# Strassen for the queries and keys of all pairs ahead of attention, with casts on GpSimd, biased exponentials in the recurrence and stored token sums for the gates

## The chip, the cores and the metric

The kernel runs on one core of a Trainium2 chip. The metric is the device time of one execution in microseconds, lower is better. The kernel before was timed in three runs, with a median of 1444.59 us (1444.48 to 1446.14).

## What is computed

The reference is one layer of a hybrid encoder on x of 1024 tokens by 1024 features, in float32. Cut to what matters:

```python
q_a, k_a, v_a, f_a, q_b, f_b, i_b, g_b, gate_a, gate_b = split(x @ w_in)
# 8 heads of 64: forgetting attention
F = cumsum(log_sigmoid(f_a + b_f), over tokens)
p = softmax(where(causal, q_a @ k_a.T / sqrt(64) + F[t] - F[s], -inf))
y_a = p @ v_a
# 4 heads of 128 x 128: gated linear recurrence, in chunks of 64 tokens
f = lb + (1 - lb) * sigmoid(f_b); k = 1 - f; b = cumsum(log f) in the chunk
S_new = exp(b_last) * S + (k * exp(b_last - b)).T @ i_b
o_b = (silu(q_b) * exp(b)) @ S + within_chunk(silu(q_b), k, b) @ i_b
y_b = rms_norm(o_b) * norm_g * sigmoid(g_b)
merged = sigmoid(gate_a) * (y_a @ w_pa) + sigmoid(gate_b) * (y_b @ w_pb)
x = layer_norm(ALPHA * x + merged @ w_o)
u, g = split(x @ w_ff_in)                    # 2 x 2816 hidden features
x = layer_norm(ALPHA * x + (silu(g) * u) @ w_ff_out)
```

## The kernel before

Every matmul operand is split into a high and a low fp32r half, and a product takes three matmuls (`mm3`: high by high, high by low, low by high). The high half is a cast on ScalarE, the low half a subtraction on VectorE (`split`). The v projection, the q and k of the first pair of heads, most of the gates and both FFN products use one level of Strassen: seven products of half size in place of eight, with sums of weights and of tokens before them and sums of results after them.

The program is not issued in the order of the code. Every call goes into `Plan`, which knows a cost for each instruction and what depends on what. `schedule` lists the calls on each engine by due times that `latest` works out backwards, `improve` repeats the two `ROUNDS` times and keeps the best, and `issue` emits a fixed order for each engine. For this reason all instructions of the profile carry one line, L363, and are told apart by the names of their tiles. SyncE issues every DMA, and its queue is such a fixed order too. Matmuls that are needed only later serve as filler: `plan.early` moves their due times, so that they can stand between those of a stage that waits on itself.

The stages, with the names of their tiles:

- The v projection by Strassen (banks `vx`, `vy`), and the forget gates (`forget_gates`, `forget_sums`), which leave the decays, running sums of log f, in DRAM (`nf_d`). The token sums of Strassen (`vops["p5"]`, `"p6"`, `"p7"`, `"p3"`, as high and low halves) are made here from x.
- q and k. `qk_first` makes pair 0 by Strassen, ahead of attention (`qk_s`, `qk_pt`). `qk_project` makes pairs 1 to 3 plainly, one after another, as filler in the attention of the pair before (`qps`, `kps`; weights `wq`, `wk`). `qk_heads` forms from a bank the tiles q2, k2 and kl of two heads: in q2 one half of the partitions holds the high part of q and the other the low part, k2 holds the high part of k twice, kl its low part.
- Attention, pair by pair. Per head, a row of decays is loaded into two quarters of `box1` (row r plain, row r+1 with the causal mask added by VectorE); two heads alternate. Scores (`s`), a softmax in 8 blocks of queries (`p`, with the sum in `soft`; GpSimd scales by the reciprocal), transposes (`pt`) and the weighted sum (`pv`). The plainly made gate columns (`gps`, `ge`) are filler here too.
- The recurrence of 4 heads (`bps` projections, `lp`, `up`, `op`, `ot`, `kdt`), `hgrn`. The forget factor `hbf` is made by a VectorE tensor_scalar, and the decayed keys `kd` from a difference with the block's total `tot` and four exponentials of 128x512.
- The gates by Strassen (`GatePair`, banks `gs`, operands `gs1` to `gs4`, weights `Tgp`). Their token sums are formed anew from x (`xg_r`) by `sums4`.
- The branch projections (`pps`), the output projection (`o`), layer norm, FFN in (`fa` to `fd`) and FFN out (`p`).

Of the kernel before, what the change touches and what calls it, by code (L numbers as in the profile page):

```python
# [34 lines left out]
ROUNDS = 20  # L35
MARGIN = 1.06
SLACK = 400.0
SWITCH = 300.0
ALPHA = 2.0 ** 0.25
# [16 lines left out]

class Plan:
# [4 lines left out]
    OWN = {"PE": 0.0, "ACT": 0.0, "DVE": 127.0, "POOL": 60.0, "SP": 2500.0}  # L62
    SETS = {AF.Exp: 0, AF.Ln: 0, AF.Sigmoid: 1, AF.Silu: 2}

    def __init__(self, tc):
        self.tc = tc
        self.calls, self.tiles, self.log, self.first = [], {}, {}, {}
        self.queues, self.rank = {}, []
        self.early = 0
        self.loose = set()  # L70

# [22 lines left out]
    def add(self, q, method, args, kw):  # L94
# [7 lines left out]
        if method == "copy_predicated":  # L102
            ins.append(outs[0])
        n = len(self.calls)
        self.rank.append(n - self.early)
        pred = set()
# [21 lines left out]
        both = sum(str(v.space).endswith("SB") and v.free_size() > 128 for v in ins) > 1  # L128
        self.calls.append((q, method, args, kw, pred, names, fresh, self.cost(q.name, method, outs, ins, kw), both))

    def cost(self, eng, method, outs, ins, kw):
# [27 lines left out]
        if eng == "POOL":  # L159
            if method == "tensor_tensor" and kw.get("op") == ALU.pow:  # L160
# [9 lines left out]
    def schedule(self, slack, wait):  # L170
# [13 lines left out]
        dma_free = 0.0  # L184
        fifo, slots = {}, {}
# [15 lines left out]
        while done < len(calls):  # L201
            best = None
            for q, av in avail.items():
                for i in av:
# [16 lines left out]
                    if not ok:  # L221
                        continue
                    if q == "ACT":
# [14 lines left out]
            if q == "SP":  # L238
                start = max(t + 100, dma_free)
                dma_free = start + d  # L240
                free[q] = t + 60
                fin = dma_free
            else:
# [6 lines left out]
                fin = t + d  # L250
                free[q] = fin
# [35 lines left out]
    def lag(self, i, u, slack):  # L287
        q, uq = self.calls[i][0].name, self.calls[u][0].name
        lat = self.OWN[q] if uq == q else self.LAT[q]
# [4 lines left out]
    def latest(self, slack):  # L294
# [7 lines left out]
        for old, i in self.after:  # L302
            for m in by.get(old, ()):
                users[m].append((i, self.LAT[calls[m][0].name] + 60))
# [29 lines left out]
    def improve(self, slack, wait):  # L334
# [4 lines left out]
        for _ in range(ROUNDS):  # L339
            last, self.rank = self.turn, self.latest(slack)  # L340
# [26 lines left out]
def trunk(ctx: ExitStack, tc, a: dict, out: bass.AP):  # L367
# [30 lines left out]
    def small(shape, name, bufs=4):  # L398
        return plan.tile(cst, shape, F32, "c_" + name, name, bufs)
# [67 lines left out]

    def operand1(tag, name):
# [3 lines left out]
    def operand4(tags, name):  # L472
        ts = [[take(tags[2 * i + j], [2, NB], f"{name}{'hl'[i]}{j}", F32R) for j in range(2)] for i in range(2)]
        return [[ts[i][c // 2][:, c % 2, :] for c in range(4)] for i in range(2)]
# [109 lines left out]
    def forget_gates():  # L584

        LO, NC = 32, KC + 4
        wfx = keep([P, NC, HA], "wfx", F32, "lnst")
# [49 lines left out]
    bf = const("bf", [NT * HA, 1])  # L637
# [29 lines left out]
    causal = const("causal", [P, 2, P], BF16, "mask")  # L667
# [40 lines left out]
    def qk_project(p):  # L708
        tiles = qk_tiles(p)
        for b in range(2):  # L710
            plan.early = AHEAD
            w = weights(a["w_qk"][b, p], [KC, P], f"w{'qk'[b]}{p}", 0)
            plan.early = 0
            for hf in range(2):
                o = bank("g", f"{'qk'[b]}ps{p}_{hf}")
                project(o, w, hf)
                qk_heads(b, hf, o, *tiles)
        return tiles

    def qk_first():  # L720

        g, u = (take("hl", [KC, P], f"w{n}0_r") for n in "qk")
        for b, t in enumerate((g, u)):
            sync.dma_start(t, a["w_qk"][b, 0])
        b11, b12, b21, b22 = g[:, :4], u[:, :4], g[:, 4:], u[:, 4:]
        t2 = take("ph", [4, P], "wqk_t2")
        p1, u2, p5 = (half("ph", f"qk0_{i}") for i in ("p1", "u2", "p5"))
        oa, ob, oc = (bank(t, f"qk0_{t}") for t in ("s", "pt", "s"))
        tiles = qk_tiles(0)

        def mul(p, src, o, first):
            T = [take(f"w{x}0" if p in ("p6", "p2", "p7") else "tt", [4, P], f"Tqk{p}{x}", F32R) for x in "hl"]
            split(*T, src)
            more = {} if first else {"skip_group_check": True}
            for c in range(4):
                mm3(o, T[0][:, c], T[1][:, c], vops[p][0][c], vops[p][1][c], first and c == 0, c == 3, more)
# [4 lines left out]
        split4(A21, a21)  # L741
        mul("p1", b11, oa, True)
        act.copy(p1, oa)
        mul("p2", b21, oa, False)
        dve.tensor_sub(t2, b22, b12)
        qk_heads(0, 0, oa, *tiles)
        mul("p6", t2, ob, True)
        dve.tensor_add(u2, ob, p1)
        mul("p3", b22, oc, False)
        dve.tensor_add(u2, oc, u2)  # L750
        qk_heads(1, 0, u2, *tiles)
# [4 lines left out]
        qk_heads(1, 1, p5, *tiles)  # L756
# [3 lines left out]
        qk_heads(0, 1, p1, *tiles)  # L760
        return tiles

    def attention(p, qk):
        q2, k2, kl = qk
        for i in range(2):
# [5 lines left out]
            for hf in range(2):  # L771
                plain, masked = (nfx[:, b0 + 4 * hf:b0 + 4 * hf + 4].rearrange("p (j c) t -> p j c t", c=2) for b0 in (0, NT))
                dve.tensor_add(masked, plain, causal[:, None].to_broadcast([P, 2, 2, P]))
# [4 lines left out]
            for qb in range(NT):  # L778
                n = (qb + 1) * P
                pt = full("pf", f"p{h}_{qb}") if qb > 3 else half("ph", f"p{h}_{qb}")  # L780
                soft = small([P, 5], "soft")
                mn, sm, rs = soft[:, :3], soft[:, 3:4], soft[:, 4:]
# [24 lines left out]
                dve.reciprocal(rs, sm)  # L807
                pool.tensor_scalar(pt[:, :n], pt[:, :n], rs, 1.0, op0=ALU.mult, op1=ALU.mult)
                pr.append(pt)
                if qb % 4 < 3:  # L810
# [26 lines left out]
    ng = const("ng", [P, 1])  # L837
    lbl = const("lbl", [P, HB])
    lbt = keep([P, 4, HB], "lbt")
# [915 lines left out]
```

## Time and profile before

| | |
|---|---|
| Median of 3 runs | 1444.59 us (1444.48 to 1446.14) |
| Span of the profiled execution, first to last instruction | 1441.5 us |
| Granted TensorE clock | 0.998 |
| TensorE matmul, busy | 1430.0 us (99%) |
| VectorE | 1112.8 us (77%) |
| ScalarE | 668.6 us (46%) |
| GpSimd | 87.2 us (6%) |
| DMA, mean over the span | 126 GB/s, 181.30 MB |

The profiled execution is one run of the program; the span leaves out what lies before its first and after its last instruction, and the median of the runs stands 3.1 us above it. A row of instructions reads: line, engine, operation, output tile <- input tiles, shapes, count | busy us in all, mean ns of one | idle time of the engine just before them, and what ended it. The engines are PE (TensorE matmul), PEld (its weight loads), DVE (VectorE), ACT (ScalarE), POOL (GpSimd) and SP (SyncE, which issues DMAs). Buffer numbers are left out of the names, so a row collects all tiles of a kind.

### The profile page before, as it was taken

What the parts mean: (1) busy time and instruction counts of PE and PEld (TensorE: products, weight loads), DVE (VectorE), ACT (ScalarE), POOL (GpSimd) and SP (SyncE); (2) the same over time, 40 slices, a digit from 0 to 9 for tenths busy, and PEclk for the clock granted to TensorE, in tenths of its full rate; (3) what the DMA queues carried; (4) which work ended last, traced back from release to release, by engine and by line L of the source; (5) the groups of instructions that cost most, each with busy time, mean ns of one, the idle gap of its engine ahead of it and who ended that gap; (6) DMA issues with size and microseconds to landing.
All of it is one profiled execution on the core that took longest, in us unless ns stands there. A gap on an engine that the chain in (4) does not pass through costs nothing.

```text
span 1441.5 us, 18901 instructions
## 1 busy us (share of the span) xinstructions
PE 1430.0 (99%) x6782; PEld 1188.2 (82%) x6782; DVE 1112.8 (77%) x1952; ACT 668.6 (46%) x1167; POOL 87.2 (6%) x100
## 2 busy tenths in 40 slices
PE   9999999999999999999999999999999999999997
PEld 7788888888888888788888888888888888888886
DVE  8998778567998999845857997666677776798596
ACT  5547768667767663344511443323333334434330
POOL 0002213120100110000000000000000000000011
PEclk9999999999999999999999999999999999999999
DMA  7022212211111455858500233233333326977632
GB/s 270 32 89 67 95 60 74 63 60 51 38 59 46 153 170 164 255 181 290 176 0 2 102 95 124 96 110 110 110 110 110 97 92 201 346 276 235 209 129 85
DMA packets 74029, 181.30 MB, mean 126 GB/s; under 512 B 8384, under 2 KB 9792, under 8 KB 73936
## 3 DMA queue, kind: packets, MB, share of 16 engines
q1 hardware_dynamic: 73936, 180.11, 37.9%
q8 instruction: 53, 0.87, 0.3%
q14 instruction: 40, 0.33, 0.1%
HBM read 139.90 MB, written 40.17 MB: 125 GB/s over the span
## 4 chain that ended last, share of the span: by engine, by line
PE 97%; DVE 2%; DMA 1%; issue 0%; ACT 0%; SPq 0%; DVEq 0%; ACTq 0%
PE p L363 14%; PE fb L363 12%; PE bps L363 9%; PE fc L363 8%; PE fa L363 8%; PE o L363 6%; PE pps L363 6%; PE gs L363 5%; PE vx L363 4%; PE gps L363 3%; PE s L363 2%; PE pv L363 2%; PE qps L363 2%; PE kps L363 2%; PE vy L363 2%; PE pt L363 2%
## 5 line engine op out<-in xcount | busy, mean ns | idle before, releaser
L363 PE MATMUL p<-dp 128*128 128x512 f32 (+1 forms) x957 | 210.1, 382 | 0.0
L363 PEld LDWEIGHTS p<-dp 128*128 128x128 f32 x957 | 175.1, 188 | 34.8
L363 PE MATMUL fc<-xs,Tp 128*128 128x512 f32 x528 | 127.3, 389 | 0.6 <-ACT Tp L363 0.6
L363 PE MATMUL fb<-xs,Tp 128*128 128x512 f32 x528 | 127.2, 389 | 0.0
L363 PEld LDWEIGHTS fc<-xs,Tp 128*128 128x128 f32 x528 | 99.1, 188 | 21.6 <-ACT Tp L363 1.0
L363 PEld LDWEIGHTS fb<-xs,Tp 128*128 128x128 f32 x528 | 99.1, 188 | 20.5
L363 PE MATMUL fa<-x,Tp 128*128 128x512 f32 x480 | 115.6, 389 | 0.0
L363 ACT CAST Tp<-t 128x512 fp32r<-128x512 f32 x88 | 54.2, 619 | 118.8 <-PE fc L363 64.8
L363 DVE TENSOR_TENSOR Tp<-t,Tp 128x512 fp32r<-128x512 f32 x88 | 60.6, 690 | 60.5 <-ACT Tp L363 59.9
L363 PEld LDWEIGHTS fa<-x,Tp 128*128 128x128 f32 x480 | 90.1, 188 | 18.7
L363 PE MATMUL bps<-xh,wb_h 128*128 128x512 f32 x192 | 76.2, 397 | 0.0
L363 PE MATMUL bps<-xl,wb_h 128*128 128x512 f32 x192 | 76.0, 396 | 0.0
L363 PE MATMUL bps<-xh,wb_l 128*128 128x512 f32 x192 | 75.5, 396 | 0.0
L363 POOL TENSOR_TENSOR norm<-norm,mhalf 128x1 f32<-128x1 f32 x16 | 17.2, 1075 | 886.3 <-DVE norm L363 886.3
L363 ACT CAST dp<-dap 128x1024 fp32r<-128x1024 f32 (+1 forms) x42 | 41.0, 979 | 57.8 <-PE p L363 35.7
L363 POOL TENSOR_SCALAR p<-p,soft 128x384 f32<-128x384 f32 (+4 forms) x64 | 51.9, 817 | 261.0 <-DVE soft L363 235.2
L363 DVE TENSOR_TENSOR tl<-pt,th 128x512 fp32r<-128x512 f32 (+1 forms) x96 | 52.2, 554 | 19.7 <-ACT th L363 15.5
L363 ACT CAST th<-pt 128x512 fp32r<-128x512 f32 (+1 forms) x96 | 45.5, 479 | 34.9 <-PE pt L363 30.8
L363 DVE TENSOR_TENSOR dp<-dap,dp 128x1024 fp32r<-128x1024 f32 (+1 forms) x42 | 47.4, 1132 | 15.9 <-ACT dp L363 15.7
L363 PE MATMUL fb<-x,Tp 128*128 128x512 f32 x240 | 57.7, 389 | 0.0
L363 PE MATMUL pt<-ident,p 128*128 128x128 f32 x288 | 53.8, 273 | 0.0
L363 ACT CAST Tp<-wg_r 128x512 fp32r<-128x512 f32 x40 | 24.9, 623 | 62.1 <-PE fb L363 30.2
(565 smaller groups left out, 3476.6 us busy)
## 6 DMA issues: line engine op xcount, KB each, us to landing
dbp<-in_w_fo SPq DMA_DIRECT2D x45, 512.0 KB, 5.3
dap<-a_d SPq DMA_DIRECT2D x35, 512.0 KB, 4.3
wg_r<-in_w_ff SPq DMA_DIRECT2D x22, 512.0 KB, 4.0
wu_r<-in_w_ff SPq DMA_DIRECT2D x22, 512.0 KB, 3.6
a_d<-ar SPq DMA_DIRECT2D x42, 256.0 KB, 2.7
a_d<-as SPq DMA_DIRECT2D x33, 256.0 KB, 3.4
wg_r<-in_w_g SPq DMA_DIRECT2D x16, 512.0 KB, 4.4
sg<-gate_d SPq DMA_DIRECT2D x32, 256.0 KB, 3.4
```

What stands on the lines that cost most here:

```text
L363: getattr(q.engine, method)(*args, **kw)
```

## The change

Six parts:

1. `qk_first` makes q and k of all four pairs by Strassen (`qk_strassen`), in the order 1, 2, 3, 0, ahead of attention. Pair 0 goes to its tiles as before. The results of pairs 1 to 3 go to DRAM (`qk_d`), each 64x512 block written twice, so that a load of 128x512 brings it to both halves of the partitions. `qk_load` reads them a pair ahead: GpSimd makes the high parts by tensor_scalar, VectorE the low parts. `qk_project` is gone.
2. The masked decay row is a load of the causal mask, now 128x1024 float32, and a DMA from GpSimd's queue that adds the decays to it in flight; VectorE's 16 additions are gone.
3. The softmax's reciprocals are taken for three blocks and then one, and the scalings are issued after them. Small constants share one tile (`few`).
4. In the recurrence ScalarE makes `hbf` with scale and bias, and the decayed keys are exponentials with the block's total as bias, 8 of 128x128 per head, without VectorE's difference.
5. The token sums of the v projection are written to DRAM (`sum_d`) and loaded again for the gates, in place of loads of x and `sums4`.
6. The planner has a cost for DMAs of GpSimd's queue, counts 500 ns for an issue on SyncE in place of 60, and runs 24 rounds with a varied slack; the first Silu of the FFN waits for the first token sums there.

The core of the diff:

```diff
-ROUNDS = 20
+ROUNDS = 24
...
-            self.rank = self.latest(slack)
+            self.rank = self.latest(slack if n < 6 else slack * vary.uniform(0, 3))
...
-                free[q] = t + 60
+                free[q] = t + 500
...
+    for n, x in enumerate((xh, xl)):
+        sync.dma_start(sum_d[0, :, n], f(x[0][:, :, hs(1)]))
+    for m, p in enumerate(("p6", "p7", "p3")):
+        for n in range(2):
+            for j in range(2):
+                sync.dma_start(sum_d[m + 1, :, n, 2 * j:2 * j + 2], f(vtiles[...][n][j]))
...
+        def put(b, hf, o):
+            if tiles:
+                return qk_heads(b, hf, o, *tiles())
+            if o is oa:
+                t = half("gt", f"qk{p}_o")
+                act.copy(t, o)
+                o = t
+            for i in range(2):
+                for j in range(2):
+                    sync.dma_start(qk_d[p, b, i, j, :, hs(hf)], o[i * DH:(i + 1) * DH])
...
+    def qk_load(p):
+        q2, k2, kl = qk_tiles(p)
+        for b in range(2):
+            for hf in range(2):
+                for i in range(2):
+                    ot = slice((1 - i) * DH, (2 - i) * DH)
+                    raw = half(f"w{'hl'[i]}0", f"qkr{p}_{b}{hf}{i}")
+                    sync.dma_start(raw, qk_d[p, b, i, :, :, hs(hf)].rearrange("j d t -> (j d) t"))
+                    if b == 0:
+                        pool.tensor_scalar(q2[i][:, hs(hf)], raw, -0.125, None, op0=ALU.mult)
+                        dve.scalar_tensor_tensor(q2[i][ot, hs(hf)], raw[ot], -0.125, f(q2[i])[ot, hs(hf)],
+                                                 op0=ALU.mult, op1=ALU.subtract)
+                    else:
+                        pool.tensor_scalar(k2[i][:, hs(hf)], raw, 1.0, None, op0=ALU.mult)
+                        dve.tensor_sub(kl[i][:, hs(hf)], raw, f(k2[i])[:, hs(hf)])
+        return q2, k2, kl
...
+        for p, w, b in ((1, "hl", 0), (2, "kb", 1), (3, "hl", 0), (0, "kb", 1)):
+            qk_strassen(p, (w, w), (("s", "pt", "s"), ("h", "pv", "h"))[b], None if p else tiles)
...
-            for hf in range(2):
-                plain, masked = (...)
-                dve.tensor_add(masked, plain, causal[:, None].to_broadcast([P, 2, 2, P]))
+            sync.dma_start(box1[:, r + 1, :], a["causal"])
+            pool.dma_start(box1[:, r + 1, :], nf_d[h].partition_broadcast(P), accum_op=ALU.add)
...
-                dve.reciprocal(rs, sm)
-                pool.tensor_scalar(pt[:, :n], pt[:, :n], rs, 1.0, op0=ALU.mult, op1=ALU.mult)
+                if qb % 4 > 1:
+                    lo = 0 if qb % 4 == 2 else 3
+                    dve.reciprocal(sums[:, 4 + lo:5 + qb % 4], sums[:, lo:1 + qb % 4])
+                    for j in range(qb - qb % 4 + lo, qb + 1):
+                        pool.tensor_scalar(pr[j][:, :w], pr[j][:, :w], rs, 1.0, op0=ALU.mult, op1=ALU.mult)
...
-        dve.tensor_scalar(fk, fk, olb[:, h:h + 1], lb[:, h:h + 1], op0=ALU.mult, op1=ALU.add)
+        act.activation(fk, fk, AF.Identity, scale=olb[:, h:h + 1], bias=lb[:, h:h + 1])
...
-            dve.tensor_sub(kd..., bw, tot...)
-            act.activation(qeb[:, odd], kd[:, odd], AF.Exp, scale=-1.0)
-            act.activation(kd[:, even], kd[:, even], AF.Exp, scale=-1.0)
+            for j in range(4):
+                for c, t in enumerate((kd, qeb)):
+                    w = blk(4 * c + j)
+                    act.activation(t[:, w], b[:, w], AF.Exp, bias=tot[:, j, c:c + 1], scale=-1.0)
...
-    gops["p6"] = operand1("m", "gs2")
-    sums4(gops["p6"], q22, q22, q11, True)
+    gops["p6"] = reload(1, "m", "gs2")
```

The planner then places everything anew. Three places show what moved.

TensorE, in attention, at the first transposes of head 1 (`pt1_0_0`). Before, the filler among them is the plain q projection of pair 1 (`qps1_1`):

```order
L363 MATMUL pt1_0_0_301<-ident_162,p1_0_288 128x128
L363 MATMUL pt1_0_0_301<-ident_162,p1_1_291 128x128
L363 MATMUL pt1_0_0_301<-ident_162,p1_2_294 128x128
L363 MATMUL pv0_1_261<-tl0_1_6_282,vhl0_218 128x256
L363 MATMUL pt1_0_0_301<-ident_162,p1_3_297 128x128
L363 MATMUL qps1_1_368<-xh0_66,wq1_h0_363 128x512
L363 MATMUL qps1_1_368<-xl0_68,wq1_h0_363 128x512
L363 MATMUL pv0_1_261<-th0_1_7_284,vhl0_218 128x128
```

After, it is the plain columns of the gates (`gps`), and the first score of head 2, from pair 1's reloaded tiles, comes 13 rows behind the last of the first four transposes:

```order
L381 MATMUL pt1_0_0_373<-ident_162,p1_3_369 128x128
L381 MATMUL pv0_1_332<-tl0_1_6_353,vhl0_287 128x256
L381 MATMUL gps0_1_0_1196<-xl0_68,wg0_1_h0_1192 128x512
L381 MATMUL pv0_1_332<-th0_1_7_355,vhl0_287 128x128
L381 MATMUL gps0_1_0_1196<-xh0_66,wg0_1_l0_1193 128x512
L381 MATMUL pv0_1_332<-tl0_1_7_356,vhl0_287 128x128
L381 MATMUL gps0_1_0_1196<-xh1_67,wg0_1_h1_1194 128x512
```

All q and k matmuls now stand ahead of the first score.

GpSimd, at head 1 of attention (`p1_*` are its softmax blocks). Before, only scalings stand there:

```order
L363 TENSOR_SCALAR p1_1_291<-p1_1_291,soft_292 128x256
L363 TENSOR_SCALAR p1_2_294<-p1_2_294,soft_295 128x384
L363 TENSOR_SCALAR p1_3_297<-p1_3_297,soft_298 128x512
L363 TENSOR_SCALAR p1_4_314<-p1_4_314,soft_315 128x640
L363 TENSOR_SCALAR p1_5_318<-p1_5_318,soft_319 128x768
```

After, casts of pair 1 (`qkr1`) and the accumulating DMA for head 2's masked row (`box1`) stand between them:

```order
L381 TENSOR_SCALAR k2_1_0_431<-qkr1_100_439 128x512
L381 TENSOR_SCALAR q2_1_1_430<-qkr1_001_436 128x512
L381 TENSOR_SCALAR p1_0_360<-p1_0_360,sums_359 128x128
L381 TENSOR_SCALAR p1_1_363<-p1_1_363,sums_359 128x256
L381 TENSOR_SCALAR p1_2_366<-p1_2_366,sums_359 128x384
L381 DMA box1_104<-nf_d_116 128x1024
L381 TENSOR_SCALAR p1_3_369<-p1_3_369,sums_359 128x512
L381 TENSOR_SCALAR k2_1_0_431<-qkr1_110_441 128x512
```

The DMA is issued behind the scaling of block 2 and its softmax sum.

VectorE, at the start of the gates (`Tgp5`, `Tgp6` are low halves of weight sums). Before, sums of tokens (`xg_r`) and low halves of them (`gs`) stand between:

```order
L363 TENSOR_TENSOR Tgp5_4l_1225<-tg1_4_1209,Tgp5_4h_1224 128x512
L363 TENSOR_TENSOR gs1_1223<-xg7_r_1202,gs1_1223 128x512
L363 TENSOR_TENSOR gs2_1228<-xg5_r_1198,gs2_1228 128x512
L363 TENSOR_TENSOR gs2_1228<-xg6_r_1200,gs2_1228 128x512
L363 TENSOR_TENSOR Tgp5_6l_1227<-tg1_6_1219,Tgp5_6h_1226 128x512
L363 TENSOR_TENSOR xg7_r_1202<-xg7_r_1202,xg3_r_1201 128x512
L363 TENSOR_TENSOR gs3l1_1238<-xg2_r_1199,gs3h1_1236 128x512
```

After, only sums and halves of weights, and work for the branch projections (`yr01`) that came forward:

```order
L381 TENSOR_TENSOR Tgp6_4l_1289<-tg2_4_1269,Tgp6_4h_1288 128x512
L381 TENSOR_TENSOR Tgp4_6l_1281<-wg6_r_1252,Tgp4_6h_1280 128x512
L381 TENSOR_TENSOR Tgp5_6l_1286<-tg1_6_1278,Tgp5_6h_1285 128x512
L381 TENSOR_TENSOR Tgp7_4l_1299<-wg5_r_1251,Tgp7_4h_1298 128x512
L381 TENSOR_TENSOR yr01_1395<-yr01_1395,yr11_1396 128x1024
L381 TENSOR_TENSOR Tgp6_6l_1292<-tg2_6_1279,Tgp6_6h_1291 128x512
```

In their place SyncE loads `gs1` to `gs4` from DRAM, each as two transfers of 1 MB (`gs3` as four of 512 KB).

More of the change, by code (lines that the diff above doesn't have):

```diff
@@ L338, in improve @@
         best = self.schedule(slack, wait), self.end, self.times
-        for _ in range(ROUNDS):
-            last, self.rank = self.turn, self.latest(slack)
+        vary = np.random.default_rng(1)
+        for n in range(ROUNDS):
+            last, self.rank = self.turn, self.latest(slack if n < 6 else slack * vary.uniform(0, 3))
             self.turn = self.rank
```

153 lines of the change are left out of this document (87 added, 66 removed).

## The prediction

> **What bounds the kernel now.** I read the page first, then the waits of TensorE, then busy times by stage, then the rows of the instructions that the change touches.
>
> ```profile
> span 1441.5 us, 18901 instructions
> ...
> PE 1430.0 (99%) x6782; PEld 1188.2 (82%) x6782; DVE 1112.8 (77%) x1952; ACT 668.6 (46%) x1167; POOL 87.2 (6%) x100
> ...
> PE 97%; DVE 2%; DMA 1%; issue 0%; ACT 0%; SPq 0%; DVEq 0%; ACTq 0%
> ```
>
> TensorE is busy in 1430.0 of 1441.5 us and carries 97% of the chain that ended last. The waits of TensorE on other engines, over the whole span, are three rows (line waited for; us in total, times, longest):
>
> ```profile
> PE vy L363 <- DVE mhalf L363: 1.2, 1, 1.2
> PE gs L363 <- DVE gu L363: 1.2, 2, 0.8
> PE fc L363 <- ACT Tp L363: 0.6, 1, 0.6
> ```
>
> One is at the start, one in the gates' products, one at the start of the FFN. So the time is the number of matmuls times what one takes, and only two things move it: fewer or more matmuls, and a wait of TensorE that goes or comes. The stages, as busy time of PE, PEld, DVE, ACT, POOL, then granted clock, DMA share, GB/s (5 to 89 us is the v projection, 89 to 112 mostly the q and k of pair 0, 112 to 324 attention, 342 to 542 the recurrence, 542 to 625 the gates):
>
> ```profile
> 5.00:89.00 84.00, 83.88 (x368) 66.14 (x367) 78.48 (x138) 42.66 (x78) 0.00 (x0) 1.00 0.39 134
> 89.00:112.00 23.00, 23.00 (x105) 18.85 (x104) 20.84 (x41) 16.08 (x29) 0.00 (x0) 1.00 0.34 116
> 112.00:324.00 212.00, 211.98 (x1150) 178.35 (x1149) 154.18 (x478) 149.53 (x324) 51.88 (x64) 1.00 0.21 69
> ...
> 342.00:542.00 200.00, 200.00 (x1096) 172.09 (x1095) 181.17 (x291) 138.93 (x261) 16.84 (x14) 1.00 0.28 91
> 542.00:625.00 83.00, 81.83 (x360) 67.19 (x359) 67.92 (x105) 27.23 (x42) 0.00 (x0) 1.00 0.64 192
> ...
> 580.00:600.00 20.00, 19.19 (x85) 15.57 (x84) 16.90 (x25) 5.41 (x8) 0.00 (x0) 1.00 0.97 269
> ```
>
> PE stands still for 0.02 us in 212 us of attention and not at all in 200 us of the recurrence, though VectorE is busy there for 181 of 200 us. VectorE at 91% (23 us of pair 0's Strassen, 20.84 busy) has not cost TensorE anything either. The clock is full everywhere, so no gain can come from it.
>
> **The matmuls that go.** A pair's q and k took 2 x 2 halves x 8 chunks x 3 terms = 96 matmuls of 128x512 in the plain way; by Strassen it is 7 products x 4 chunks x 3 terms = 84. Pair 0 was made so already; for pairs 1 to 3 that is 288 against 252, 36 fewer. What one costs is read from unbroken runs on the chain (start, duration, count):
>
> ```profile
> 103.42 2.72 PE qk_pt L363 x12
> ...
> 211.19 10.88 PE kps L363 x48
> ```
>
> 2.72/12 and 10.88/48 are both 0.2267 us, so a Strassen matmul is as dear as a plain one, and 36 x 0.2267 = **8.16 us** less. No other TensorE work is added: the two copies of the result, the loads and the casts are for other engines. If the old 288 matmuls had covered something that now shows, the cost is a new wait; that is the rest of the sum.
>
> **Ahead of attention.** Three pairs more are made there, 3 x 84 x 0.2267 = 57 us. One pair asks of VectorE 7 low halves, 4 sums of weights and 5 sums of results, 16 instructions at about 0.69 (the kl row below), 11 us beside 19 us of matmuls, which is lighter than what the 89 to 112 row ran without a gap. The order puts matmuls of the next pair into the places where a pair would wait for its own sums. What can be late is the weights: SyncE now issues 8.4 MB of token sums and 6.3 MB of q and k into DRAM here, 14.7 MB. The first row moved 134 GB/s at a share of 0.39, so the full rate is about 134/0.39 = 344 GB/s, and 14.7 MB are 43 us of it, an estimate, in some 100 us that had over 0.6 free. It fits, but weights queued behind these writes may land late: 0 to 2 us. The written data is read much later; its own lateness costs nothing here.
>
> **Attention.** 288 filler matmuls (65.3 us) leave it, and gate matmuls take their place. By the order, TensorE has 159 us of work from the first score to the last weighted sum (212 - 65.3, and 12 us of gate matmuls that moved in). VectorE loses and gains:
>
> ```profile
> L363 DVE TENSOR_TENSOR box<-box,causal 128x512 f32<-128x512 f32 x16 | 10.8, 694 | 0.1
> ...
> L363 DVE RECIPROCAL soft<-soft 128x1 f32<-128x1 f32 x64 | 10.0, 158 | 4.8 <-ACT p L363 4.5
> ...
> L363 DVE SCALAR_TENSOR_TENSOR q<-qps,q 64x512 fp32r<-64x512 f32 x12 | 8.3, 688 | 2.5 <-ACT q L363 2.3
> L363 DVE TENSOR_TENSOR kl<-kps,k 64x512 fp32r<-64x512 f32 x12 | 8.2, 688 | 15.7 <-ACT k L363 15.6
> ...
> L363 DVE TENSOR_TENSOR wk_l<-wk_r,wk_h 128x512 fp32r<-128x512 f32 x6 | 4.7, 778 | 6.7 <-ACT wk_h L363 6.6
> ...
> L363 DVE TENSOR_TENSOR wq_l<-wq_r,wq_h 128x512 fp32r<-128x512 f32 x6 | 4.1, 688 | 0.7 <-ACT wq_h L363 0.6
> ...
> L363 POOL TENSOR_SCALAR p<-p,soft 128x512 f32<-128x512 f32 x8 | 5.9, 733 | 4.8 <-DVE soft L363 3.5 <-PE pt L363 1.0 <-PE s L363 0.3
> ```
>
> Off VectorE go 10.8 (masked rows), 8.3 + 8.2 (halves of q and k), 4.7 + 4.1 (weights' low halves) and 32 x 0.158 = 5.1 (reciprocals, now batched): 41 us. On come 24 low halves at 0.688 = 16.5. So 154.2 - 41 + 16.5 = 130 us in 159, 82% where it was 73%. GpSimd gets 24 casts at 0.733 = 17.6, with 51.9 makes 69 us of 159. Neither is at its end.
>
> But the two engines get in each other's way. In the timeline (start, duration; both inputs of the DVE instructions in SBUF):
>
> ```profile
> 146.01 2.26 POOL L363 TENSOR_SCALAR p<-p,soft 128x896 f32<-128x896 f32 x2 [1.21 <-PE pt L363]
> ...
> 147.59 1.22 DVE L363 TENSOR_TENSOR wk_l<-wk_r,wk_h 128x512 fp32r<-128x512 f32 x1
> ...
> 197.11 1.13 POOL L363 TENSOR_SCALAR p<-p,soft 128x1024 f32<-128x1024 f32 x1 [0.54 <-DVE soft L363]
> 197.46 1.32 DVE L363 TENSOR_TENSOR vhl<-va,vhl 128x512 fp32r<-128x512 f32 x1 [0.23 <-ACT vhl L363]
> ```
>
> These took 1.22 and 1.32 us where wq_l, the same shape, takes 0.688: 0.53 and 0.63 longer, and each ends 0.54 us after the GpSimd instruction beside it does. The Trainium skill ("SBUF — State Buffer", section "Who interferes with whom") has the rule: a DVE instruction with two SBUF inputs contends with a GpSimd instruction that reads SBUF, and the second to start blocks fully. By that rule, with which these two rows agree, the change makes such meetings more frequent. From the rows alone: the 24 casts read SBUF, and the 24 new low halves take both inputs from SBUF where the old kl had one in PSUM. If each of the 24 meets a GpSimd instruction, that is 24 x 0.6 = 14 us more for VectorE: 144 of 159, 91%, the load that the recurrence carried without a gap. I take 1 us of it as reaching TensorE; bounds 0 and 14.
>
> The masked row of a head is now a load of the big mask and an accumulating DMA from GpSimd. The nearest row:
>
> ```profile
> box<-nf_d SPq DMA_DIRECT2D x8, 512.0 KB, 4.1
> xg_r<-in_xT SPq DMA_DIRECT2D x8, 512.0 KB, 5.3
> ```
>
> By the order, the DMAs of heads 3 to 7 stand 13 to 15 us of matmuls ahead of their first use, that of head 2 about 5. No row shows an accumulating DMA. At 4.1 head 2 just makes it; at twice that, 8.2, it waits 3 us. I take 0, bounds 0 and 3. The Trainium skill ("DMA: Bandwidth & Descriptors", section "Anatomy of one DMA — SWDGE (gpsimd) path") gives about 2.0 us plus bytes/436 GB/s, an estimate of 3.2 us for 512 KB; no run here shows it, and by it nothing waits.
>
> **Recurrence.** The rows of what moves:
>
> ```profile
> L363 DVE TENSOR_TENSOR kd<-hbb,tot 128x1024 f32<-128x1024 f32 x4 | 4.9, 1216 | 0.0
> ...
> L363 DVE TENSOR_SCALAR hbf<-hbf,lbt 128x1024 f32<-128x1024 f32 x4 | 3.2, 809 | 2.3 <-ACT hbf L363 2.3
> ...
> L363 ACT ACTIVATE p<-p,soft 128x1024 f32<-128x1024 f32 x8 | 9.2, 1154 | 0.5 <-DVE soft L363 0.5
> ...
> L363 ACT ACTIVATE p<-p,soft 128x128 f32<-128x128 f32 x8 | 3.2, 400 | 0.1
> ...
> L363 ACT ACTIVATE kd<-kd 128x512 f32<-128x512 f32 x4 | 2.5, 632 | 0.0
> ```
>
> VectorE loses 4.9 + 3.2 = 8.1 us of its 181. ScalarE gains per head one 128x1024 (1.15) and 8 exponentials of 128x128 (8 x 0.400 = 3.2) in place of two of 128x512 (2 x 0.632): 3.1 us, 12 in all, from 139 to 151 of 200. PE had no wait here, so nothing is gained; I take 0, bounds 0 and 3 (one head's 3.1 us showing once).
>
> **Gates.** 32 instructions of VectorE and 16 casts go:
>
> ```profile
> L363 DVE TENSOR_TENSOR xg_r<-xg_r 128x512 f32<-128x512 f32 x16 | 10.7, 683 | 0.7 <-DMA xg_r<-in_xT 0.7
> ...
> L363 DVE TENSOR_TENSOR gs<-xg_r,gs 128x512 fp32r<-128x512 f32 x12 | 7.9, 681 | 0.0
> ```
>
> 16 sums and 16 low halves at 0.68 are 21.8 us, most of them ahead of and within the gates. That relieves VectorE in the stretch where TensorE waited twice for gu, in all **1.2 us**, which I count as gone. In exchange the loads double, 8.4 MB of stored sums for 4.2 MB of x: 4.2 MB at the 269 GB/s of the 580 to 600 row are 16 us more of DMA, and the second half of the operand of p6 stands on SyncE behind stores that wait for their data, at about the time of its need: 0 to 4 us, taken as 0. The 0.6 us at fc stays: the first Silu only comes later. The FFN's matmuls are untouched.
>
> **The sum.** 1441.5 - 8.16 - 1.2 + 1.0 = 1433.1 us of span. The median of the runs, 1444.59, stands 3.1 above the profiled span; so 1433.1 + 3.1 = **1436.2 us**. About 0.2% (2.9 us) is what a measurement of this kernel can tell from no change: faster is below 1441.7, slower above 1447.5.
>
> **Rivals.**
>
> *VectorE becomes the bound of attention (slower).* It would have 144 us in 159 with every cast in its way, and every head's chain of score, softmax, transpose and weighted sum passes through it and GpSimd, with 65 us less filler to hide behind. If the 0.6 us of all 24 reach TensorE, 1435.2 + 14.4 = 1449.6 us. It decides from 12.3/0.6, over 20 of the 24; or, put otherwise, from 1.5 us lost by each of 8 heads. For it: the two timeline rows. Against: the 342 to 542 row, 91% without a gap, and that each cast comes a pair ahead of its use. Chance 0.13.
>
> *The accumulating DMA is slow.* At 10 us, head 2 waits 5: 1436.2 + 5 = 1441 us; only past 14 us do all later heads wait too. For it: no row shows its like, and GpSimd issues it between scalings that wait for the softmax. Against: the plain load of the same bytes, 4.1. Chance 0.08.
>
> *The reload comes late.* The gates' p6 and p5 wait 4 us for stored sums: 1436.2 + 4 = 1440 us. For it: the DMA share of 0.97. Against: the loads start in the recurrence, with a share of 0.28. Chance 0.10.
>
> *The change does not give its matmuls back.* The 8.16 us turn into gaps because, ahead of attention and in the recurrence, TensorE catches up with VectorE and ScalarE: 1444.6 - 1.2 = 1443.4 us, the same. Against: VectorE is relieved by 8 us in the recurrence and by 22 at the gates, where the gaps would lie. Chance 0.07.
>
> **How the numbers follow.** The forecast has the remaining 0.62 with its own range of 1433.5 (no new wait and the fc wait gone too, 1434.6, with 1 us of scatter) to 1440. The cases below 1441.7 are the forecast, the late reload and most of the slow DMA: 0.78 faster. The same: 0.07 and the worst of these two, 0.09. Slower: 0.13. The range 1433.5 to 1445.0 leaves out the slower rival, and with it and some scatter not more than 2 in 10.
>
> **What would show it.** Right: 36 fewer matmuls at 0.2267; no row over 1 us among TensorE's waits in attention and at the gates; a span near 1433. The rivals: low halves kl and q of 1.2 us and more, with waits of pt or s for them; waits of s for DMA box at head 2; waits of gs for DMA gs; PE gaps from 85 to 161 us. I am wrong if the waits of TensorE add up to more than 6 us in place of 3, or if matmuls of another line run longer than 0.2267 us each.

## The result, and the profile after

The kernel after takes 1450.73 us in the median of 20 runs (1446.14 to 1455.77), before 1444.82 in as many (1442.93 to 1449.08): 1.0035 times as long, 95% interval 1.0026 to 1.0045. It is 5.9 us slower; 8.6 us less was forecast.

The page of after, and the waits of TensorE that are above those of before:

```profile
span 1449.1 us, 18963 instructions
...
PE 1428.0 (99%) x6746; PEld 1184.7 (82%) x6746; DVE 1099.7 (76%) x1900; ACT 648.2 (45%) x1147; POOL 129.1 (9%) x132
...
PE 92%; DMA 3%; DVE 1%; POOL 1%; ACT 1%; issue 1%; SPq 0%; DVEq 0%; POOLq 0%; ACTq 0%
```

```profile
PE op L381 <- DVE ob L381: 3.8, 1, 3.8
PE gs L381 <- DVE gu L381: 2.0, 1, 2.0
PE pt L381 <- DVE tl L381: 1.5, 1, 1.5
PE pt L381 <- POOL p L381: 1.4, 3, 0.7
...
PE gs L381 <- DMA gs<-sum_d: 1.1, 1, 1.1
```

In these rows `op` and `ob` are the output of the recurrence, in its bank and then scaled, and `ot` its transposes; `gu` and `gp` are sums of the gates' products, `yr` a sum of two loads of attention's output, `kl` the low half of k, and `th` and `tl` the halves of a transposed softmax block.

The 36 matmuls are gone (6782 records to 6746), and still the span is longer. TensorE's busy share hides where, since a matmul that runs slowly is busy too. So I take from each trace the start of every matmul and subtract from the step to the next what it takes in an unbroken run (0.2267 us for 512 columns, 0.173, 0.120 and 0.108 for 384, 256 and 128); the rest is lost time, in us, by stage (attention from the first `s`, recurrence from the first `lp`, gates from behind the last `lp` to the first `pps`). Full rate alone is 1418.9 us before and 1410.7 in every kernel with the Strassen q and k, 8.2 less as forecast. Lost time is not all waits: in before's attention no wait is listed, and its 3.5 us are steps that are each less than 0.2 us too long.

| profiled execution | span | start, v | q, k | attention | recurrence | gates | rest | lost |
|---|---|---|---|---|---|---|---|---|
| before | 1441.5 | 3.0 | 0.2 | 3.5 | 2.2 | 2.1 | 1.6 | 12.7 |
| after | 1449.1 | 3.4 | 0.1 | 7.0 | 3.0 | 13.5 | 1.3 | 28.4 |

15.7 more lost against 8.2 saved is 7.5, the 7.6 between the spans. Attention has 3.5 of it, the gates 11.4.

**The gates.** Three windows of after (busy PE, PEld, DVE, ACT, POOL, clock, DMA share, GB/s), the longest DMA waits on the chain (start, length), what VectorE waited for, and the rows of VectorE and TensorE at the first stand:

```profile
520.00:540.00 20.00, 16.21 (x76) 13.77 (x75) 10.07 (x19) 6.03 (x22) 2.32 (x2) 0.83 0.85 232
540.00:560.00 20.00, 18.95 (x87) 15.38 (x86) 12.32 (x18) 7.41 (x12) 0.00 (x0) 1.00 1.03 347
560.00:580.00 20.00, 17.37 (x69) 13.00 (x67) 13.73 (x22) 4.05 (x6) 0.00 (x0) 0.91 0.83 243
```

```profile
516.56 13.84 DMA yr<-ya_d
...
540.24 11.06 DMA yr<-ya_d
```

```profile
DVE yr L381 <- DMA yr<-ya_d: 10.9, 3, 5.3
...
DVE gu L381 <- DMA yb_d<-yb: 2.7, 1, 2.7
```

```profile
530.50 1.23 DVE L381 TENSOR_TENSOR yr<-yr,yr 128x1024 f32<-128x1024 f32 x1 [5.31 <-DMA yr<-ya_d]
531.64 0.68 DVE L381 TENSOR_TENSOR ob<-op,ss 128x512 f32<-128x512 f32 x1
...
532.38 0.80 PE L381 MATMUL op<-vbm,at 128*128 128x128 f32 x2 [3.79 <-DVE ob L381]
...
537.02 0.63 PE L381 MATMUL gs<-xl,Tgp_4h 128*128 128x512 f32 x1
```

The sum `yr` belongs to the branch projections, which begin 90 us later. It was the token sums from x that had kept its buffers (`wr0`, `wr1`, the home of `xg0` and `xg4`) and so its loads back; without them the planner issues the loads at 516 us, among the stored sums. They take 13.84 us to land. VectorE, which takes its instructions in the order issued, stands 5.31 us at `yr`; `ob` stands behind it, and TensorE waits 3.8 us for `ob`. Then TensorE comes back at a clock of 0.83 over that window, with 512-column steps of 0.43 us in place of 0.227 until 538 us: of the 6.9 us lost between 520 and 540, 3.95 are the wait and 3 the slow restart. The second stand, at 561 us, costs 2.2 and is followed by five slow matmuls, in the window with a clock of 0.91. It has another cause. VectorE stands 2.74 us at a `gu` whose buffer still holds a `yb`, and the store of that `yb` landed only 9.9 us after its issue:

```profile
553.17 9.86 DMA yb_d<-yb
563.06 0.70 DVE gu L381
```

The late store is in every kernel with stored sums. In those seven (after, e2, e3, e4, e7, e12, e15) the slowest store of a `yb` landed in 9.9 to 13.9 us, in the eleven without in 4.1 to 6.5; in five of the seven `gu` waited for it, 1.9 to 4.3 us.

**Attention.** GpSimd's rows, VectorE's low halves, and one place:

```profile
L381 POOL TENSOR_SCALAR q<-qkr 128x512 fp32r<-128x512 f32 x12 | 19.6, 1639 | 7.5 <-DMA qkr<-qk_d 7.5
L381 POOL TENSOR_SCALAR k<-qkr 128x512 fp32r<-128x512 f32 x12 | 19.3, 1633 | 4.4 <-DMA qkr<-qk_d 4.4
...
L381 POOL TENSOR_SCALAR p<-p,sums 128x512 f32<-128x512 f32 x8 | 6.2, 780 | 0.4 <-PE pv L381 0.4
```

```profile
L381 DVE SCALAR_TENSOR_TENSOR q<-qkr,q 64x512 fp32r<-64x512 f32 x12 | 9.7, 805 | 0.6 <-POOL q L381 0.4
L381 DVE TENSOR_TENSOR kl<-qkr,k 128x512 fp32r<-128x512 f32 x12 | 9.6, 804 | 1.3 <-POOL k L381 1.3
```

```profile
184.36 1.92 POOL L381 TENSOR_SCALAR k<-qkr 128x512 fp32r<-128x512 f32 x1
186.25 1.49 POOL L381 TENSOR_SCALAR q<-qkr 128x512 fp32r<-128x512 f32 x1
187.72 1.92 POOL L381 TENSOR_SCALAR p<-p,sums 128x128 f32<-128x128 f32 x3
```

```profile
186.31 1.09 DVE L381 TENSOR_TENSOR kl<-qkr,k 128x512 fp32r<-128x512 f32 x1 [1.30 <-POOL k L381]
187.77 0.68 DVE L381 SCALAR_TENSOR_TENSOR q<-qkr,q 64x512 fp32r<-64x512 f32 x1 [0.37 <-POOL q L381]
188.38 1.27 DVE L381 TENSOR_TENSOR tl<-pt,th 128x512 fp32r<-128x512 f32 x2
```

A cast to fp32r takes 1.49 us in the median and 1.64 in the mean, twice a scaling of the same shape in float32 (0.70 and 0.78). Two of them stand ahead of head 1's first scalings. The way to TensorE here goes over VectorE's order: it stands 1.30 us at `kl` for the cast of k and 0.37 at the low half of q for the cast of q, `tl` comes behind them, and TensorE's transposes wait 1.5 us for `tl` and lose 1.67. At 0.733 us, the price of the prediction, the cast of k would have ended 1.2 us sooner.

### The profile page after: what moved, and what is told of

Same layout as the page of the kernel before. It is cut to its first block, busy times and chain, and to the rows that moved or that the text cites. A ratio compares the mean times of both kernels' runs of the same rounds, so it can differ in the third digit from the quotient of the medians.

```text
span 1449.1 us, 18963 instructions
## 1 busy us (share of the span) xinstructions
PE 1428.0 (99%) x6746; PEld 1184.7 (82%) x6746; DVE 1099.7 (76%) x1900; ACT 648.2 (45%) x1147; POOL 129.1 (9%) x132
## 4 chain that ended last, share of the span: by engine, by line
PE 92%; DMA 3%; DVE 1%; POOL 1%; ACT 1%; issue 1%; SPq 0%; DVEq 0%; POOLq 0%; ACTq 0%
PE p L381 14%; PE fb L381 12%; PE bps L381 9%; PE fc L381 8%; PE fa L381 8%; PE o L381 6%; PE pps L381 6%; PE gs L381 5%; PE vx L381 3%; PE vy L381 2%; PE gps L381 2%; PE pv L381 2%; PE s L381 2%; PE pt L381 2%; DMA yr<-ya_d 2%; PE qk_s L381 2%
## 5 line engine op out<-in xcount | busy, mean ns | idle before, releaser
L381 PEld LDWEIGHTS fb<-xs,Tp 128*128 128x128 f32 x528 | 99.1, 188 | 20.5
L381 POOL TENSOR_TENSOR norm<-norm,few 128x1 f32<-128x1 f32 x16 | 14.9, 933 | 890.2 <-DVE norm L381 890.2
L381 DVE TENSOR_TENSOR tl<-pt,th 128x512 fp32r<-128x512 f32 (+1 forms) x96 | 52.2, 551 | 12.3 <-ACT th L381 10.3
L381 POOL TENSOR_SCALAR p<-p,sums 128x128 f32<-128x128 f32 (+3 forms) x64 | 53.3, 847 | 45.6 <-DVE sums L381 16.8
L381 PE MATMUL pt<-ident,p 128*128 128x128 f32 x288 | 50.9, 273 | 2.9 <-DVE tl L381 1.5
L381 ACT ACTIVATE p<-p,soft 128x640 f32<-128x640 f32 (+4 forms) x64 | 49.9, 781 | 6.5 <-DVE soft L381 6.0
```

The costliest lines, as they stand in the source:

```text
L381: getattr(q.engine, method)(*args, **kw)
```

## The experiments

The lost time by stage, as above. The medians are of many runs and the stages of one, so the two can differ by some us: e2's profile fell on its quickest run, 4.6 us below its median, those of e5 to e8 on their slowest. Each edit also makes the planner place the whole program anew, so a difference of a few us between two kernels is not the edited instructions alone; e14 below shows how much that can be.

| | median us | ratio to before (95%) | attention | gates | lost |
|---|---|---|---|---|---|
| after | 1450.73 | 1.0035 (1.0026, 1.0045) | 7.0 | 13.5 | 28.4 |
| e1 sums from x | 1443.96 | 0.9991 (0.9982, 1.0000) | 9.2 | 3.8 | 21.8 |
| e2 yr later | 1447.52 | 1.0017 (1.0006, 1.0029) | 8.6 | 5.1 | 20.5 |
| e3 before, stored sums | 1450.49 | 1.0040 (1.0025, 1.0055) | 4.1 | 6.4 | 17.5 |
| e4 casts on ScalarE | 1448.36 | 1.0023 (1.0014, 1.0032) | 7.6 | 11.5 | 25.8 |
| e9 before, planner | 1445.29 | 1.0003 (0.9994, 1.0013) | 3.4 | 3.6 | 14.2 |
| e10 before, q and k | 1448.88 | 1.0028 (1.0017, 1.0038) | 8.9 | 7.1 | 24.8 |
| e11 e10, casts on ScalarE | 1444.18 | 0.9995 (0.9986, 1.0004) | 4.9 | 8.3 | 21.7 |
| e12 masks on VectorE | 1450.43 | 1.0040 (1.0026, 1.0053) | 9.3 | 12.3 | 28.9 |
| e13 e1, casts on ScalarE | 1442.50 | 0.9981 (0.9968, 0.9993) | 5.4 | 8.9 | 21.2 |
| e15 e2, casts on ScalarE | 1448.29 | 1.0017 (1.0007, 1.0027) | 6.9 | 10.0 | 25.8 |
| e16 e13, ge held | 1449.38 | 1.0033 (1.0021, 1.0046) | 14.5 | 4.8 | 26.2 |

**e1: no stored sums.** The stores to `sum_d` and its loads go; the loads of x and `sums4` come back.

```diff
-    gops["p6"] = reload(1, "m", "gs2")
+    gops["p6"] = operand1("m", "gs2")
+    sums4(gops["p6"], q22, q22, q11, True)
```

> The kernel after with the gates' token sums formed from x again as before; nothing is written to sum_d or loaded from it. In the profile of after TensorE loses 13.2 us against full rate between 520 and 580 us, where before lost 2.0 around its gates, and 3.5 us more than before in attention. Theory A (VectorE stands at the first sum yr, whose loads were issued early into the traffic of the stored sums, and op and gs wait behind it) and theory B (8.4 MB of stored sums are too much traffic there, whoever waits): both 11 us less, about 1439.5 us. Theory C (VectorE and GpSimd in each other's way, or the longer row of work ahead of attention): under 2 us less, 1449 us or more.

The gates lose 3.8 in place of 13.5 and the median falls by 6.8 us, where theories A and B expected 11: the stored sums are most of what the gates lose. It does not reach 1439.5, as attention loses 9.2 in this order and the start 1.4 more than in after.

**e2: yr later.** `gated` is the last matmul of the first p6.

```diff
+                        plan.behind = (gated,) if c == 0 else ()
                         sync.dma_start(t[j * DH:(j + 1) * DH], src[c, j, a_])
+                        plan.behind = ()
```

> The kernel after, with one edit: the loads of the first yr are issued only behind the gates' first product p6, as late as before had them; the stored sums stay. Theory A: op no longer waits for ob, and of the 13.2 us lost at the gates about 3 stay (1.1 of them waiting for the stored sums): 1440.5 us. Theory B: the same 8.4 MB still come in the same stretch, gs waits for them or for weights, and the time is within 2 us of after's 1450.7.

No wait of `op` for `ob` is left, and 3.2 of e1's 6.8 us are won: theory A explains about half. VectorE still stands 5.3 us at the later `yr`, and the rest is not in this profile of the quickest run; e15's, of a run at its median, has it.

**e3: before with stored sums.** The reverse of e1's edit, made to before.

> The kernel before with the stored token sums alone (written ahead of attention, loaded for the gates); q and k, casts, masks, recurrence and planner as before. By its order the first sum yr then stands ahead of ob on VectorE as in after. Theories A and B: slower than before by about 11 us, 1456 us, with op or gs waiting between 520 and 590 us. Theory C: 1.2 us faster, 1443.6 us.

5.7 us slower than before's 1444.82, half of what was expected and of the sign that A and B give. So the stored sums cost about 6 us with either q and k. Its profile shows the same two links as after's first stand:

```profile
PE ot L363 <- DVE ob L363: 2.6, 1, 2.6
...
DVE yr L363 <- DMA yr<-ya_d: 6.2, 3, 3.8
```

**e4: casts on ScalarE.**

```diff
-                        pool.tensor_scalar(k2[i][:, hs(hf)], raw, 1.0, None, op0=ALU.mult)
+                        act.copy(k2[i][:, hs(hf)], raw)
```

> The kernel after with the 24 casts of the reloaded q and k on ScalarE in place of GpSimd. Theory D (in attention GpSimd, which works in order, stands at a cast that waits for its load, and scalings and transposes wait behind it): the 3.5 us lost in attention go, and the gates stay as they are: 1447 us. Rival E (the accumulating DMA or VectorE's own load is what attention waits for): within 1 us of after.

2.4 us less, but attention still loses 7.6, with one stand of 2.6 us behind a `kl` that waits for its cast, and here the cast waits for its load (ScalarE stands 2.9 us at it). The loads of q and k take 5.3 us to land, 5.4 in after, where e11 has 3.0. So late loads are a second cause in this order, and by itself e4 left the cause in attention open.

**e5 to e8: the planner's numbers.** The planner has 0.67 us for a cast, and 358 GB/s and 2.5 us for a transfer.

```diff
-                return n * 0.833 + 244
+                return n * (2.42 if o.dtype == F32R else 0.833) + 244
...
-        return float(o.nbytes()) / 358.0
+        return float(o.nbytes()) / 260.0
```

> The kernel of e1 (token sums formed from x) with one number of the planner changed: a GpSimd tensor_scalar that writes fp32r is planned at 1.48 us, as the trace of after shows it where undisturbed, in place of 0.67. In the profile of e1 TensorE loses 9.2 us in attention against 3.5 before, with VectorE standing at kl and q until a cast is done. Theory F (the casts are twice as long as planned, so VectorE is put at kl and q too early and stands there): attention loses about 4, 1439.5 us. Theory G (the casts start late because their loads land late): no change, 1444 us. Theory H (the casts and low halves themselves are too much for the stretch, wherever they are put): no change or worse.

> The kernel of e5 with the planner also counting transfers on SyncE at 260 GB/s and 3.5 us until they land, in place of 358 GB/s and 2.5. Theory F: as e5, within 1 us. Theory G: attention loses about 4 only here, 1439.5 us, and e5 stays at 1444. Theory H: 1444 us or more here too.

> The kernel after, with these two corrections of the planner's numbers alone (casts 1.48 us, transfers 260 GB/s and 3.5 us); the stored sums stay. By its order the first sum yr now stands behind the first ob on VectorE. Theory A with F or G: the gates lose 5 in place of 13.5 us, attention 4 in place of 7: 1439.5 us. Theory B (too much traffic): the gates lose over 9 us, 1446 us or more.

> The kernel of e1 with the 24 casts on ScalarE (0.63 us each in e4) and the planner's transfers at 260 GB/s and 3.5 us. Theory F: 1439.5 us, as no cast is longer than planned. Theory G: the same, as loads are planned as late as they are. Theory H for GpSimd alone: also 1439.5 us. If attention still loses over 6 us, none of the three holds and the row of work in attention (no filler of q and k left) is what costs.

All four were slower than expected by every theory that names a gain: 1448.78, 1452.34, 1453.17 and 1451.40 us. With the cast's true time alone (e5) attention loses 7.9; with later transfers too it loses 6.2 (e6) and, with the casts on ScalarE, 4.7 (e8), but these transfers' numbers move the whole program: start and v lose 7 and 9 us in place of 3.4 and the FFN 3.6 and 4.5 in place of 0.9. In e7, with the stored sums, the gates still lose 9.4, as theory B has it, and TensorE waits 5.1 us at one place for the stored sums themselves. In e5 the gates lose 13.8 with no stored sums at all; VectorE stands at weights here, and 4.3 of the 13.8 lie ahead of the last matmul of the recurrence (more on this at e10):

```profile
DVE tg L381 <- DMA wg_r<-in_w_g: 5.8, 2, 3.7
```

So theory F falls as put: a right price in the planner does not make room for the casts. G is not settled by these. e5 shows too that a stand at the gates is not tied to one load: `yr` in after, weights here.

**e9: before with the planner's changes alone**, the first lines of the diff.

> The kernel before with the planner's changes alone (24 rounds with a varied slack, 500 ns for an issue on SyncE); every instruction is as before, only their order differs. In all eight new orders so far TensorE lost 17 to 32 us against full rate, in before's own order 12.7. Theory I (any new order of this program loses more, since the planner's costs differ from the chip's and VectorE stands at what is late): 5 us or more slower than before, 1450 us. Theory J (the loss belongs to what the change adds): within 2 us of before, 1443 to 1447 us.

The same as before. Theory I falls as put: this new order of the old instructions does not lose more. It is one new order, and says nothing of how much the orders of the changed program differ.

**e10 and e11: before with the Strassen q and k alone**, the casts on GpSimd and on ScalarE.

```diff
-            qk = qk_project(p + 1)
+            qk = qk_load(p + 1)
```

> The kernel before with the first part of the change alone: q and k of all pairs by Strassen ahead of attention, through DRAM, with the casts on GpSimd. Masks, softmax, recurrence, gates and planner as before. 36 matmuls fewer are 8.2 us. Theory J with the casts to blame in attention: attention loses 7 to 9 in place of 3.5, the gates 2 to 4: 1441.5 us. Theory I: 1448 us or more. The prediction's own sum for this part: 1436.5 us.

> The kernel of e10 with the 24 casts on ScalarE (0.63 us each in e4) in place of GpSimd (1.63 in after). If the long casts are what attention loses by: 4 us less than e10, 1437.5 us. If VectorE's stand at late loads is: as e10.

The clearest pair. Part 1 by itself makes the kernel 4.1 us slower in spite of 8.2 us less of matmuls; with the casts on ScalarE it is as quick as before, 4.7 us less, and attention loses 4.9 in place of 8.9. The rows of e10 show a way from GpSimd to TensorE, the late scalings, a wait that e11 has not:

```profile
L363 POOL TENSOR_SCALAR k<-qkr 128x512 fp32r<-128x512 f32 x12 | 20.2, 1684 | 1.4 <-DMA qkr<-qk_d 1.3
```

```profile
PE pt L363 <- POOL p L363: 3.3, 2, 2.1
```

The loads land in 3.2 and 3.0 us in the two, so late loads are not it here. The size depends on the order: the same move of the casts gave 2.4 us from after to e4, 1.5 from e1 to e13, and cost 0.8 from e2 to e15. The gates lose 7.1 and 8.3, without stored sums and with before's gates. Of this, 4.7 us lie in both between the last `lp` and the last matmul of the recurrence (`op`, `ot`), where before loses 0.2: 4 of the 96 partial gate columns `ge` are left to stand there, 27 in before, and 48 have gone into attention.

**e12: masks on VectorE.**

```diff
-            sync.dma_start(box1[:, r + 1, :], a["causal"])
-            pool.dma_start(box1[:, r + 1, :], nf_d[h].partition_broadcast(P), accum_op=ALU.add)
+                dve.tensor_add(masked, plain, causal[:, None].to_broadcast([P, 2, 2, P]))
```

> The kernel after with the masked decay rows added by VectorE again (16 additions of 0.69 us) and no accumulating DMA, which took 7.1 us to land where 4.1 was reckoned. No wait of TensorE or VectorE in after names that DMA, so theories A and F: 1450 us, within 2 us of after. Theory E (GpSimd's queue is held by it and the scalings are late): attention loses 4 in place of 7 us, 1447 us.

No change in the time, as expected, and no wait of after names the accumulating DMA: it costs nothing that TensorE sees. Attention loses 9.3 in this order, by the casts again: two of them (3.35 us) stand ahead of scalings at 203 us, the transposes wait 2.5 us for scalings in all, and 3.4 us at half the clock follow.

**e13 to e16: both repairs, and what is left.**

> The kernel after with the two repairs at once: token sums formed from x (e1) and the 24 casts on ScalarE (e11 against e10 gave 4.7 us). Theories A or B with F's long casts, and nothing else of weight: attention loses 5 in place of 7 to 9 us, the gates 3.8 in place of 13.5; the span is 1410.7 of matmuls, some 16 lost and 8.8 behind the last, 1436 us, 1438.5 us with what lies around it. If the batched softmax or the other parts cost too, or the filler that attention has taken from the recurrence: 1442 us or more.

> The kernel of e13 with the masked rows on VectorE again. By e12 the accumulating DMA costs nothing: within 1.5 us of e13. If the GpSimd queue is cleaner without it, up to 2 us less.

> The kernel of e2 (stored sums kept, first yr issued later) with the casts on ScalarE. Theory A alone: as e13, 1438.5 us. Theory B (the reload's traffic costs beyond yr): 3 us or more above e13.

e13 is the quickest kernel of the study, 1442.50 us, and beats before by 0.1 to 0.3%. It is 4 us above its expectation: attention loses 5.4 as expected, the gates 8.9 in place of 3.8. e15, with the stored sums and late yr, is 5.8 us above e13: the reload costs beyond the early yr, as theory B has it. What VectorE meets there is the late store of after's second stand:

```profile
DVE gu L381 <- DMA yb_d<-yb: 4.3, 1, 4.3
```

e14 came out at 1449.21 (ratio 1.0021, 1.0011 to 1.0031), 6.7 us above e13; its attention loses the same 5.2, its gates 10.6, and why the 16 additions should cost so much here and nothing in e12 is not settled. It warns against reading any single pair to the last us.

e16 holds the partial gate columns back (`done` is the last matmul of attention):

```diff
+        plan.behind = (done,)
         w = weights(a["w_g"][i, fb], [KC, P], f"we{n}", lane)
+        plan.behind = ()
```

> The kernel of e13 with the partial gate columns ge (96 matmuls, 21.8 us) held until attention's matmuls are done; in after and its kin 24 to 48 of them are used up as filler in attention, in before none. Theory K (the 288 matmuls of q and k were filler, and attention pays for them with filler that the end of the recurrence then lacks): the stretch from the last lp to pps loses 2 in place of about 4 us, and attention, with 20 to 40 fillers less, loses more: 1 to 4 us above e13 or equal. If attention doesn't miss them: 2 us below e13.

Counted in the traces between the first `s` and the last `pv`, attention has 520 filler matmuls in before, 319 in after, 324 in e13 and 269 in e16; of `ge`, 0, 31, 36 and 19 of 96 stand ahead of the recurrence's first `lp`. With the 55 fewer, attention loses 14.5 in place of 5.4 us and the median rises by 6.9, more than the 1 to 4 that were expected. The other kernels with the casts on ScalarE fit: with 348 filler matmuls attention loses 4.7 to 5.2 (e8, e11, e14), with 324 it loses 5.4 to 7.6 (e4, e13, e15). And 14.5 lies far outside the 4.7 to 9.3 of all other kernels with the Strassen q and k, whatever their order. So the first half of theory K holds: attention needs filler, and the q and k had been it.

The second half, that what attention takes is missing at the end of the recurrence, e16 shows less well. Its gates lose 4.8 in place of 8.9, but only 0.8 of these 4.1 us lie ahead of the last matmul of the recurrence; the rest lies in the products behind it. Better evidence is the 4.7 us of e10 and e11, and 4.1 and 4.3 in e14 and e5, where 48 `ge` had gone too; with 19 to 36 gone and no stored sums (e1, e13, e16) it is 0.3 to 1.1.

## Why the prediction was wrong

The sum failed at two terms. Attention was put at 1.0 us more and the gates at 1.2 us less; in the profiles they lost 3.5 and 11.4 us more. The terms one by one:

- **The matmuls that go**: right. 1418.9 to 1410.7 us at full rate, 8.2 where 8.16 was worked out.
- **Ahead of attention**: right. The new stretch of q and k loses 0.1 us, so weights were not late there.
- **Attention, the casts' price**: wrong. 0.733 us was taken from the float32 scaling of the same shape; the casts write fp32r and took 1.64, 38.9 us for 24 in place of 17.6. The scalings stand behind them on GpSimd and `tl` behind the low halves on VectorE; taking them off GpSimd was worth 4.7 us from e10 to e11, 2.4 and 1.5 in two other pairs and nothing in the fourth. The prediction's "I take 1 us of it" looked only at the lock. The lock is there, but small: the low halves took 0.805 where 0.688 was reckoned, 24 x 0.117 = 2.8 us of VectorE and not 14. VectorE was busy for 150 of attention's 179 us, 84% where 82 was worked out, so it was not the bound.
- **Attention, the filler**: the term that was left out in kind. The prediction noted that 288 filler matmuls leave, and priced their leaving at nothing, and the gate matmuls that move in at nothing too (it counted 12 us of them; `gps`, `ge` and `bps` grew by 96, 21.8 us). Filler taken out of a stage that waits on itself has a price: e13 to e16, 55 fewer, 9.1 us in attention. The end of the recurrence loses with what attention takes, 4.7 us in e10 and e11. How much of after's own loss this is was not separated.
- **The accumulating DMA**: right in its effect, no wait names it and e12 shows no change in the time, though it landed in 7.1 us, not in the 4.1 of the nearest row or the 3.2 of the estimate beside it.

```profile
box<-nf_d POOLq DMA_DIRECT2D x8, 512.0 KB, 7.1
...
yr<-ya_d SPq DMA_DIRECT2D x16, 256.0 KB, 10.2
```

- **Recurrence**: nearly right, 0.8 us more lost where 0 was taken of bounds 0 and 3.
- **Gates**: wrong. 1.2 us of gain and 0 of cost were taken, bounds 0 and 4; the stored sums cost 6.8 us (after to e1) and 5.7 put into before (e3), and 11.4 more are lost in the profiled gates. The late reload was a rival, at the right place and with the right cause (traffic; the share was 1.03 between 540 and 560 us), at 1440 us; but it looked at one victim only. TensorE waited 1.1 us for the stored sums in after, 5.1 in e7. What stood in after was VectorE, at a load that the change does not name, moved ahead because a buffer had come free, and at a `gu` behind a store that landed late. And the price of a stand lacked the slow restart, 3 us behind a wait of 3.95.
- **The slower rival** named VectorE's lock in attention, 1449.6 us. The time came near that, by another way: attention lost 3.5 more, not 14.4. That it came near is luck.
- **The rival that the matmuls are not given back**, 1443.4 us, is what e11 shows of part 1 alone (1444.18): 8.2 us of matmuls gone and as much lost again. It looked ahead of attention and in the recurrence; the gaps lay in attention, at the recurrence's end and in the gates.
- **The prediction's own sign of being wrong** came: the listed waits of TensorE in after add up to 12.3 us, where it named 6.

## What to carry to other kernels

Matmuls that a waiting stage uses as filler may not be saved by their full time when they go: count what fills the stage afterwards, and what that filler leaves uncovered where it stood before. When a change frees a buffer, look which load moves up into it, and which instruction in which in-order queue then waits for that load, with all that stands behind it; and which buffers wait for a store in the same traffic. Price an instruction by a row with the same output type, not only the same shape and engine. Where every edit moves the whole order, try it in more than one surrounding: moving the casts was worth 4.7, 2.4, 1.5 and -0.8 us in four.

## What the runs showed that was not expected

A tensor_scalar of 128x512 on GpSimd took 1.64 us into fp32r and 0.78 into float32. A stand of TensorE of 3.95 us was followed by 5.6 us of matmuls at half rate (0.43 us for 512 columns), which cost 3 us more; a stand of 2.2 us by five of them. The traces' own record of the granted clock says the same: 0.5 from 531.2 to 538.0 us and for 3.4 us from 565.4. Over all 18 traces between 20 and 1300 us, half the clock came behind each of the nine stands of 2.5 us and more, three of the eight between 2.0 and 2.5 us, and none of the thirteen between 1.5 and 2.0; twice it came behind shorter stands close together (0.85 and 1.20 us in e12). It lasted 3.41 or 6.83 us each time. The Trainium skill ("TensorE: Matmul & The Clock Gate", section "Part 1: The HAM clock gate (the "warmup" mystery)") gives half the clock after an idle window of about 3.4 us, until TensorE has been busy for as long; the first stand agrees, and so do the lengths of 3.41 us and twice that; but the second, shorter than the window, was followed by slow matmuls too, 1.5 us after work had begun again, and so were others from 2.07 us on. Accumulating DMAs of 512 KB landed in 7.1 us, plain loads of the same rows and size in 5.5 in the same trace. Beside the stored sums a store of 256 KB landed in up to 13.9 us, without them in at most 6.5.
